# Gate and up projections of two feed-forward layers computed with seven block products

## The chip, the cores and the metric

The kernel runs on 1 core of one Trainium2 chip. The metric is the device time of one execution in microseconds (us). Three runs of the kernel before took 1439.99, 1441.54 and 1442.35 us; their median is 1441.54 us.

## The reference, cut to what matters

One layer of a hybrid decoder on 544 tokens (512 of a new sequence, 8 sequences of 4 new tokens): a half-step feed-forward layer, a mixer, a second half-step feed-forward layer, a gated per-layer embedding, a last norm. All of it is float32.

```python
def _swiglu(h, w_up, w_down):
    g, u = jnp.split(h @ w_up, 2, axis=-1)
    return (jax.nn.silu(g) * u) @ w_down

x = x + 0.5 * _swiglu(_rmsnorm(x, n_f1), w_f1u, w_f1d)      # w_up 1024 x 5632, w_down 2816 x 1024
m, new_conv, new_ssm, new_hg = _mixer(_rmsnorm(x, n_mix), ...)
x = x + m
x = x + 0.5 * _swiglu(_rmsnorm(x, n_f2), w_f2u, w_f2d)
gate = jax.nn.sigmoid(_rmsnorm(x, n_ple) @ w_ple_gate)
e = _rmsnorm(p @ w_ple_proj, ple_post)                      # p has 256 features
x = x + gate * e
y = _rmsnorm(x, norm_final)
```

The mixer also returns new recurrent states of the 8 sample sequences (`new_ssm`, `new_hg`): 32 blocks of 128x512 in, as many out.

## The kernel before

Tokens lie along the free dimension: x is held as 8 tiles of 128 features x 544 tokens, and a product's output is 128 features x 544 tokens in two PSUM banks of 272 columns each, the two halves. A float32 product is made of three matmuls in the reduced type: with a = hi + lo, it is hi·hi + hi·lo + lo·hi (`mm6`, L133: six matmuls of 272 columns for a 128x128 block of weights, three kinds by two halves). So every weight slab (`slab`, L117: one transfer of 512 KB into `wraw`) costs a cast on ScalarE (`whi`, L124) and a subtraction on VectorE (`wlo`, through `tt`, L54), both 128x1024, and every activation is split in the same way.

A feed-forward layer (`ffn`, L197) goes over 22 pairs j of a gate block and an up block. Each of the two is one slab, 8 blocks, 48 matmuls, so a pair has 96 matmuls into two `ps_up` tiles of the PSUM pool `big` (two tiles of two banks). Then VectorE multiplies both by the inverse norm r (`ft`), ScalarE does Silu, VectorE multiplies, and the product is split into `hh` and `hl`. All 22 pairs stay in SBUF; then the down projection (`ps_dn`) goes over 8 output tiles m with 22 blocks each in one PSUM sum, and adds half of it to x. A second PSUM pool, `sm` (4 banks, `ps_s`), serves small products.

Feed-forward layer 1 starts with the product of the per-layer embedding, `ps_e` (96 matmuls, from L280), made while x is loading; e is normed beside the up pairs (`e_sq`, `e_out`) and spilled to `es_d` in DRAM. In the mixer, input projections are `ps_in`, the output projection `ps_wo` (L791: 8 tiles m of 2 slabs). The updates of sample states (`ssm_update` L799, `hg_update` L832) are handed to the second layer's `ffn` as `extra` and run beside its up pairs. At the end come the gate's products (`ps_pg` and `ps_s`, L939; the first half of the columns for all m, then the second; `gh` and `gl` are the hi and lo parts of its weights) and the last norm (`final`, L895).

The code is recorded in program order and a scheduler then puts each engine's instructions in an order. Each engine, and SyncE's queue of transfers (SP), works through its own list in that order.

## Time and profile before

| | |
|---|---|
| median of 3 runs | 1441.54 us |
| profiled execution | span 1439.4 us |
| PE busy | 1421.3 us, 99% |
| DVE, ACT, POOL busy | 797.4, 542.1, 84.2 us (55, 38, 6%) |
| DMA | 159.43 MB, mean 111 GB/s |
| chain that ended last | PE 96%, of the span `ps_up` 37%, `ps_in` 22%, `ps_dn` 18%, `ps_wo` 6% |
| `ps_up` matmuls | 4224 in all (1408 of each of three kinds) |

The span is the time from the first to the last record of the profiled execution; the median of the runs is 2.1 us above it. PE is TensorE's matmuls, DVE is VectorE, ACT is ScalarE, POOL is GpSimd. Matmuls overlap in their pipeline, so the duration of one record (some 290 ns) is longer than its share of a chain.

### The profile page before, as it was taken

How to read it: one execution, taken by the hardware profiler on the slowest of the kernel's cores; microseconds unless marked ns; L12 is line 12 of the kernel's file. 1: busy time of each engine (PE TensorE's matmuls, PEld its weight loads, DVE VectorE, ACT ScalarE, POOL GpSimd, SP SyncE). 2: the span in 40 equal slices, each digit the busy share in tenths (PEclk: the TensorE clock that was granted, in tenths of full speed). 3: DMA queues.
4: the chain of work that ended last, by engine and by line, in shares of the span. 5: the costliest groups of instructions: out<-in, count | busy, mean ns of one | idle time of the engine just before them, and what ended most of it. 6: DMA issues, size and time to landing. Idle time of an engine off the chain costs nothing.

```text
span 1439.4 us, 26883 instructions
## 1 busy us (share of the span) xinstructions
PE 1421.3 (99%) x11461; PEld 1380.7 (96%) x11461; DVE 797.4 (55%) x1351; ACT 542.1 (38%) x841; POOL 84.2 (6%) x110
## 2 busy tenths in 40 slices
PE   8999999999999999999999999999999999999997
PEld 7999999999999999999999879999999999999997
DVE  6444544423237787777777466255676764322264
ACT  7322322222234355555555345233222222222264
POOL 2000000000101200000001021100000000000000
PEclk9999999999999999999999999999999999999998
DMA  6222422233331242322222352234455553232421
GB/s 212 89 88 88 136 89 88 85 91 114 114 121 60 90 137 92 92 92 90 92 91 99 98 173 74 88 107 125 163 191 168 169 176 96 81 96 81 142 90 63
DMA packets 58824, 159.43 MB, mean 111 GB/s; under 512 B 7568, under 2 KB 12816, under 8 KB 58704
## 3 DMA queue, kind: packets, MB, share of 16 engines
q1 hardware_dynamic: 57120, 155.10, 33.6%
q10 hardware_dynamic: 1584, 2.61, 0.5%
q8 instruction: 90, 1.47, 0.4%
q14 instruction: 30, 0.25, 0.1%
HBM read 140.93 MB, written 16.75 MB: 110 GB/s over the span
## 4 chain that ended last, share of the span: by engine, by line
PE 96%; ACT 1%; DVE 1%; DMA 1%; issue 0%; SPq 0%; DVEq 0%; ACTq 0%
PE ps_up L137 37%; PE ps_in L137 22%; PE ps_dn L137 18%; PE ps_wo L137 6%; PE ps_s L939 3%; PE ps_s L522 1%; PE ps_s L519 1%; PE ps_pg L939 1%; PE ps_s L499 1%; PE ps_s L632 1%; PE ps_s L495 1%; PE ps_s L162 0%; DMA x<-in_xT 0%; PE ps_s L170 0%; PE ps_s L648 0%; PE ps_s L644 0%
## 5 line engine op out<-in xcount | busy, mean ns | idle before, releaser
L124 ACT CAST whi<-wraw 128x1024 fp32r<-128x1024 f32 (+2 forms) x207 | 213.0, 1029 | 713.1 <-PE ps_up L137 305.4
L54 DVE TENSOR_TENSOR wlo<-wraw,whi 128x1024 fp32r<-128x1024 f32 (+2 forms) x207 | 248.5, 1200 | 173.4 <-ACT whi L124 170.5
L137 PE MATMUL ps_up<-xwl,whi 128*128 128x272 f32 x1408 | 292.3, 289 | 0.0
L137 PE MATMUL ps_up<-xwh,whi 128*128 128x272 f32 x1408 | 291.8, 288 | 0.3 <-ACT e L288 0.2
L137 PE MATMUL ps_up<-xwh,wlo 128*128 128x272 f32 x1408 | 291.5, 288 | 0.0
L137 PEld LDWEIGHTS ps_up<-xwh,whi 128*128 128x128 f32 x1408 | 222.7, 188 | 2.0 <-ACT e L288 0.5
L137 PEld LDWEIGHTS ps_up<-xwl,whi 128*128 128x128 f32 x1408 | 222.0, 189 | 0.0
L137 PEld LDWEIGHTS ps_up<-xwh,wlo 128*128 128x128 f32 x1408 | 220.3, 188 | 0.0
L54 DVE TENSOR_TENSOR ft<-ps_up,r 128x544 f32<-128x544 f32 x88 | 63.7, 724 | 230.3 <-PE ps_up L137 222.7
L137 PE MATMUL ps_in<-xwh,whi 128*128 128x272 f32 x832 | 183.6, 298 | 0.0
L137 PE MATMUL ps_in<-xwh,wlo 128*128 128x272 f32 x832 | 175.6, 291 | 0.0
L137 PE MATMUL ps_in<-xwl,whi 128*128 128x272 f32 x832 | 175.1, 290 | 0.0
L137 PEld LDWEIGHTS ps_in<-xwh,whi 128*128 128x128 f32 x832 | 132.4, 189 | 8.5 <-issue 8.2
L137 PEld LDWEIGHTS ps_in<-xwh,wlo 128*128 128x128 f32 x832 | 131.5, 188 | 2.9 <-issue 2.9
L137 PE MATMUL ps_dn<-hl,whi 128*128 128x272 f32 x640 | 132.9, 289 | 0.0
L137 PEld LDWEIGHTS ps_in<-xwl,whi 128*128 128x128 f32 x832 | 131.3, 189 | 1.5 <-issue 1.5
L137 PE MATMUL ps_dn<-hh,wlo 128*128 128x272 f32 x640 | 132.6, 289 | 0.0
L137 PE MATMUL ps_dn<-hh,whi 128*128 128x272 f32 x640 | 132.4, 288 | 0.0
L137 PEld LDWEIGHTS ps_dn<-hh,wlo 128*128 128x128 f32 x640 | 100.8, 188 | 0.0
L137 PEld LDWEIGHTS ps_dn<-hh,whi 128*128 128x128 f32 x640 | 100.6, 188 | 0.0
L137 PEld LDWEIGHTS ps_dn<-hl,whi 128*128 128x128 f32 x640 | 100.3, 188 | 0.0
L54 POOL TENSOR_TENSOR sq<-sq 128x544 f32<-128x544 f32 x16 | 23.7, 1481 | 818.3 <-ACT sq L74 818.3
(323 smaller groups left out, 1852.9 us busy)
## 6 DMA issues: line engine op xcount, KB each, us to landing
wraw<-in_w_in SPq DMA_DIRECT2D x52, 512.0 KB, 3.4
wraw<-in_w1u SPq DMA_DIRECT2D x44, 512.0 KB, 3.3
wraw<-in_w2u SPq DMA_DIRECT2D x44, 512.0 KB, 3.4
wraw<-in_w1d SPq DMA_DIRECT2D x16, 512.0 KB, 3.5
h<-in_hssm SPq DMA_DIRECT2D x32, 256.0 KB, 2.9
wraw<-in_w_o SPq DMA_DIRECT2D x16, 512.0 KB, 3.8
wraw<-in_w2d SPq DMA_DIRECT2D x16, 512.0 KB, 3.5
s<-in_hhg SPq DMA_DIRECT2D x8, 512.0 KB, 3.7
```

Source lines behind the costliest of these rows:

```text
L54: (eng or V).tensor_tensor(out=out, in0=a, in1=b, op=op)
L124: A.copy(hi[:, s], raw[:, s])
L137: PE.matmul(ps[:m, hf, :HN], w, x[:, hf * HN:(hf + 1) * HN], start=start and n == 0, stop=stop and n == 2)
L495: PE.matmul(pi[32 * j:32 * j + 32], Cm[:, b], h0, start=b % 2 == 0, stop=b % 2 == 1, tile_position=(0, 32 * j))
L499: PE.matmul(pst, Bk, xef, start=True, stop=True)
L519: PE.matmul(py[64 * e:64 * e + 64, q * P:q * P + n], xdt[:n, 2 * q + e], E[:n, 2 * q + e, :n], start=True, stop=pi is None, tile_position= ...
L522: PE.matmul(py[:, q * P:q * P + n], yf[:, q * P:(q + 1) * P], cs("sel") if smpl else cs("ident"), start=False, stop=True)
L632: PE.matmul(pat[32 * j:32 * j + 32, c * P:(c + 1) * P], cw[:, c * P + 32 * j:c * P + 32 * j + 32], qs, start=True, stop=True, tile_positio ...
L939: PE.matmul(ps[:, :HN], w[k // 4][:, k % 4 * P:k % 4 * P + P], xw[k][x][:, sl], start=k == 0 and n == 0, stop=k == KD - 1 and n == 2)
```

## The change

Of 22 pairs the first (`up_plain`) is computed as before. For each of the others the gate and up blocks, [1024 features] x [128 gate, 128 up], and the activations, [544 tokens] x [1024 features], are seen as 2x2 blocks (features in two halves of 512, tokens in two halves of 272), and the four block sums come from seven block products instead of eight. A product is 4 blocks of three matmuls, 12 matmuls of 272 columns.

Sums and differences of blocks are needed on both sides. Of the activations (`strassen_x`): t1 to t4 on POOL, once per layer. Of the weights (`strassen_w`), for every pair: `wr1[4:8]` = r1 + r3 (POOL, 512 wide), `wsf` = r1 − r2 (DVE, 1024 wide), `wr3[4:8]` = r2 − sf (POOL, 512 wide), and hi and lo parts of r2, of `wr1[4:8]`, of `wsf` and of r3. On the result side ACT copies partial sums out of PSUM (`keep`: s1, s5, s2, s3, 272 wide), and DVE and POOL add. The products run through four banks of the pool `sm`, and the last product of a pair (`rest`) is put behind the second of the next.

The down projection is done in groups, after pairs 6, 12, 18 and at the end (6, 6, 6 and 4 pairs), each a PSUM sum of its own that is added to x. The embedding product e and its norm stand behind layer 2 instead of before layer 1, and the spill is gone. The state updates stand in the loop of `ps_wo`, two for each of 16 slabs.

```diff
-    def ffn(xs, nname, wu, wd, fp, pre, acc=None, extra=()):
-                for k in range(KD):
-                    mm6(ps, hi[:, k], lo[:, k], xw[k][0], xw[k][1], k == 0, k == KD - 1)
...
+    def strassen_w(src, fp, plain=False):
+        r1 = fp.tile([P, 8, P], F32, name="wr1", tag="wr1", bufs=2)
+        r2 = wp.tile([P, 8, P], F32, name="wraw", tag="wraw", bufs=2)
+        r3 = fp.tile([P, 8, P], F32, name="wr3", tag="wr3", bufs=2)
+        sf = fp.tile([P, 8, P], F32, name="wsf", tag="wsf", bufs=1)
+        nc.sync.dma_start(r2, src[:, 4:12])
+        nc.sync.dma_start(r1[:, 0:4], src[:, 0:4])
+        nc.sync.dma_start(r3[:, 0:4], src[:, 12:16])
...
+        g1 = cut(r2, wp, "")
...
+        tt(r1[:, 4:8], r1[:, 0:4], r3[:, 0:4], ALU.add, eng=G)
+        g2 = cut(r1[:, 4:8], fp, "2", 4, bufs=1)
+        tt(sf.rearrange("p (a b) c -> p a (b c)", a=2), r1.rearrange("p (a b) c -> p a (b c)", a=2),
+           r2[:, 0:4].rearrange("p b c -> p (b c)").unsqueeze(1).to_broadcast([P, 2, 512]), ALU.subtract)
+        g3 = cut(sf, fp, "3", bufs=2)
+        tt(r3[:, 4:8], r2[:, 4:8], sf[:, 4:8], ALU.subtract, eng=G)
+        g4 = cut(r3, wp, "")
+        return {1: (g1, 0), 2: (g1, 4), 5: (g2, 0), 7: (g3, 0), 6: (g3, 4), 4: (g4, 0), 3: (g4, 4)}
+
+    def product(ps, w, x, start):
+        (hi, lo), o = w
+        for k in range(4):
+            xh, xl = x[k // 2]
+            for n, (a, b) in enumerate(((lo, xh), (hi, xh), (hi, xl))):
+                PE.matmul(ps[:, :HN], a[:, o + k], b[:, k % 2], start=start and k == 0 and n == 0,
+                          stop=k == 3 and n == 2, skip_group_check=not start)
...
+        def up(j):
+            w = strassen_w(wu[j], fp)
+            a, e = small(), small()
+            product(a, w[1], X[1], True)
+            s1 = keep(a, "s1")
...
+            product(e, w[5], X[5], True)
+            s5 = keep(e, "s5")
+            while late:
+                late.pop()()
+            d = small()
+            product(d, w[2], X[2], True)
+            g = fp.tile([P, T], F32, name="g", tag="g", bufs=2)
+            tt(g[:, :HN], s1, d[:, :HN], ALU.add)
+            product(a, w[6], X[6], False)
+            s2 = keep(a, "s2")
+            product(e, w[3], X[3], False)
+            tt(g[:, HN:], s2, e[:, :HN], ALU.add)
+            r = rr[0]
+            tt(g, g, r, ALU.mult)
+            sg = g
+            act(sg, g, AF.Silu)
+            tt(sg, sg, r, ALU.mult, eng=G)
+            product(a, w[7], X[7], False)
+            s3 = keep(a, "s3")
+            tt(s5, s5, s3, ALU.add, eng=G)
+
+            def rest():
+                product(a, w[4], X[4], False)
+                tt(sg[:, :HN], sg[:, :HN], a[:, :HN], ALU.mult)
+                tt(sg[:, HN:], sg[:, HN:], s5, ALU.mult)
+                hh = fp.tile([P, T], F32R, name="hh", tag="h")
+                hl = fp.tile([P, T], F32R, name="hl", tag="h")
+                A.copy(hh, sg)
+                tt(hl, sg, f32(hh), ALU.subtract)
+                hs.append((hh, hl))
...
+        for j in range(1, NFF):
+            up(j)
+            if j and j % 6 == 0:
+                down(s0, j - s0)
+                s0 = j
...
+                    for g in begun:
+                        next(g, None)
+                    begun = [x() for x in ups[:2]]
+                    del ups[:2]
+                    for g in begun:
+                        next(g)
                 tt(h2(xt), ps[:, :, :HN], h2(xt), ALU.add)
...
+    with tc.tile_pool(name="f3", bufs=34, reuse_waits="tile") as fp:
...
+            ps = big.tile([P, 2, 512], F32, name="ps_e", tag="big")
...
+            e = eslot("e")
+            A.copy(h2(e), ps[:, :, :HN])
+            es.append(e)
```

**VectorE and GpSimd in the up phase.** Of the kernel before, one pair on VectorE in layer 1 (`ft` is a gate or up block, `hl` the split of their product):

```order
L54 TENSOR_TENSOR ft_1047<-ps_up_943,r_372 128x544
L54 TENSOR_TENSOR wlo_1117<-wraw_1115,whi_1116 128x1024
L54 TENSOR_TENSOR ft_1050<-ps_up_998,r_372 128x544
L54 TENSOR_TENSOR ft_1050<-ft_1047,ft_1050 128x544
L54 TENSOR_TENSOR wlo_1185<-wraw_1183,whi_1184 128x1024
L54 TENSOR_TENSOR hl_1054<-ft_1050,hh_1053 128x544
```

With the change, one pair on VectorE in the steady part of layer 1 (`g` is the pair's gate, later its product with up; `wsf`, `wr1`, `wr3` are raw weights and their sums):

```order
L54 TENSOR_TENSOR wlo_1812<-wr3_1791,whi_1811 128x1024
L54 TENSOR_TENSOR g_1742<-s2_1756,ps_s_1682 128x272
L54 TENSOR_TENSOR g_1742<-g_1742,r_318 128x544
L54 TENSOR_TENSOR g_1742<-g_1742,s5_1709 128x272
L54 TENSOR_TENSOR wlo3_1941<-wsf_1926,whi3_1940 128x1024
L54 TENSOR_TENSOR wsf_2060<-wr1_2057,wraw_2058 128x1024
L54 TENSOR_TENSOR wlo2_1936<-wr1_1923,whi2_1935 128x512
L54 TENSOR_TENSOR g_1742<-g_1742,ps_s_1681 128x272
L54 TENSOR_TENSOR wlo_1931<-wraw_1924,whi_1930 128x1024
L54 TENSOR_TENSOR hl_1860<-g_1742,hh_1859 128x544
L54 TENSOR_TENSOR g_1876<-s1_1829,ps_s_1863 128x272
```

and on GpSimd, over the same pair (the last row begins the next):

```order
L54 TENSOR_TENSOR g_1742<-g_1742,r_318 128x544
L54 TENSOR_TENSOR s5_1709<-s5_1709,s3_1786 128x272
L54 TENSOR_TENSOR wr1_2057<-wr1_2057,wr3_2059 128x512
L54 TENSOR_TENSOR wr3_2059<-wraw_2058,wsf_2060 128x512
L54 TENSOR_TENSOR g_1876<-g_1876,r_318 128x544
```

VectorE has eleven instructions to a pair where it had six, and GpSimd four where it had none: the gate's second product by r, after Silu, the sum s5 + s3 and two sums of raw weights. The weights' rows are those of the two pairs that follow. On ScalarE the copy s2, which the product M7 (into the same bank) waits for, stands behind `hh` of the pair before and behind a cast of weights.

**VectorE from the output projection into layer 2.** Before, around the last addition of `ps_wo` to x (`xwl` is the lo part of the activations):

```order
L57 SCALAR_TENSOR_TENSOR xwl_10507<-xb_9573,vec_67,xwh_10506 128x544
L57 SCALAR_TENSOR_TENSOR xwl_10511<-xb_9573,vec_67,xwh_10510 128x544
L54 TENSOR_TENSOR wlo_10589<-wraw_10587,whi_10588 128x1024
L57 SCALAR_TENSOR_TENSOR xwl_10515<-xb_9573,vec_67,xwh_10514 128x544
L54 TENSOR_TENSOR xb_9573<-ps_wo_10352,xb_9573 128x544
L54 TENSOR_TENSOR wlo_10663<-wraw_10661,whi_10662 128x1024
L54 TENSOR_TENSOR sq_10463<-sq_10463,sq_10483 128x544
L57 SCALAR_TENSOR_TENSOR xwl_10519<-xb_9573,vec_67,xwh_10518 128x544
```

With the change:

```order
L54 TENSOR_TENSOR xb_9844<-ps_wo_11017,xb_9844 128x544
L54 TENSOR_TENSOR h0_11080<-h0_11080,ps_s_11157 128x512
L54 TENSOR_TENSOR s0_11095<-s0_11095,ps_s_11161 128x512
L54 TENSOR_TENSOR h0_11165<-h0_11165,ps_s_11179 128x512
L54 TENSOR_TENSOR s0_11170<-s0_11170,ps_s_11183 128x512
L54 TENSOR_TENSOR sq_11187<-sq_11187,sq_11207 128x544
L165 RECIPROCAL ra_11411<-ra_11411 128x5
L61 TENSOR_SCALAR b11_11227<-xb_9844,vec_67 128x272 x2
L54 TENSOR_TENSOR bl_11231<-b11_11227,bh_11230 128x544
L54 TENSOR_TENSOR b12l_11238<-b12_11234,b12h_11237 128x544
L61 TENSOR_SCALAR b11_11243<-xb_9844,vec_67 128x272 x2
L54 TENSOR_TENSOR wlo2_11299<-wr1_11287,whi2_11298 128x512
```

The splits of activations stood among the last tiles of `ps_wo`; now every block of layer 2 (`b11`, `b12h`, `bl` and, further on, those of b21, b22 and t1 to t4) stands behind the last state update.

**ScalarE at the end.** Before, around the gate's weights:

```order
L74 ACTIVATE sq_14884<-xb_9573 128x544
L883 CAST gh_14906<-wraw_14910 128x512
L883 CAST gh_14907<-wraw_14910 128x512
L883 CAST gh_14916<-wraw_14920 128x512
L883 CAST gh_14917<-wraw_14920 128x512
L883 CAST gh_15011<-wraw_15015 128x512
L883 CAST gh_15012<-wraw_15015 128x512
L74 ACTIVATE xwh_14859<-xb_9573,vec_67 128x544
L883 CAST gh_15055<-wraw_15059 128x512
```

With the change, the same place:

```order
L1033 COPY e_15691<-ps_e_15678 128x544
L74 ACTIVATE sq_15927<-e_15661 128x544
L74 ACTIVATE sq_15930<-e_15676 128x544
L1033 COPY e_15706<-ps_e_15693 128x544
L74 ACTIVATE sq_15933<-e_15691 128x544
L74 ACTIVATE sq_15935<-e_15706 128x544
L1033 COPY e_15721<-ps_e_15708 128x544
L74 ACTIVATE sq_15938<-e_15721 128x544
L1033 COPY e_15736<-ps_e_15723 128x544
L74 ACTIVATE sq_15941<-e_15736 128x544
L1057 CAST gh_15944<-wraw_15948 128x512
```

The copies of `ps_e` out of PSUM, one for each of 8 tiles, and the squares of e now stand between the casts of the gate's first slabs and those of the others.

## Rows read from the trace of the kernel before

**Rows 1.** The chain of waits on the page (part 4): shares of the span by engine.
```profile
PE 96%; ACT 1%; DVE 1%; DMA 1%; issue 0%; SPq 0%; DVEq 0%; ACTq 0%
```

**Rows 2.** Windows: window, length, busy us of each engine (count), PEclk, DMA share, GB/s.
```profile
0.00:21.00 21.00, 14.21 (x96) 13.54 (x96) 13.07 (x18) 15.50 (x24) 0.45 (x6) 1.00 0.73 264
964.00:1240.00 276.00, 275.48 (x2160) 273.89 (x2159) 170.97 (x291) 81.14 (x107) 0.00 (x0) 1.00 0.47 151
1240.00:1374.00 134.00, 134.00 (x1064) 134.00 (x1064) 39.98 (x45) 34.86 (x44) 8.18 (x6) 1.00 0.35 106
1374.00:1439.40 65.40, 55.28 (x440) 54.86 (x438) 38.39 (x87) 36.39 (x72) 2.70 (x2) 0.93 0.19 65
```

**Rows 3.** Chain of waits in order of time: start us, length us, what.
```profile
4.50 6.39 DMA x<-in_xT
...
21.06 7.55 PE ps_up L137 x58
...
291.31 132.96 PE ps_dn L137 x1056
...
963.79 6.05 PE ps_up L137 x48
...
1240.60 133.27 PE ps_dn L137 x1056
1373.88 6.70 PE ps_pg L939 x53
...
1389.92 16.27 PE ps_s L939 x130
```

**Rows 4.** DVE groups by form; after the bar: busy us, mean ns of one, idle before.
```profile
L54 DVE TENSOR_TENSOR wlo<-wraw,whi 128x1024 fp32r<-128x1024 f32 x189 | 231.9, 1227 | 172.8 <-ACT whi L124 169.8
L54 DVE TENSOR_TENSOR ft<-ps_up,r 128x544 f32<-128x544 f32 x88 | 63.7, 724 | 230.3 <-PE ps_up L137 222.7 <-ACT r L173 7.3
...
L54 DVE TENSOR_TENSOR gt<-gt,e 128x272 f32<-128x272 f32 x16 | 6.9, 439 | 4.0 <-ACT gt L74 3.7
```

**Rows 5.** DVE timeline in the first 21 us; first column is the start.
```profile
12.96 0.72 DVE L54 TENSOR_TENSOR sq<-sq 128x544 f32<-128x544 f32 x1
13.59 0.78 DVE L57 SCALAR_TENSOR_TENSOR xwl<-x,vec,xwh 128x544 fp32r<-128x544 f32 x1
...
19.37 1.22 DVE L54 TENSOR_TENSOR wlo<-wraw,whi 128x1024 fp32r<-128x1024 f32 x1
20.50 0.78 DVE L57 SCALAR_TENSOR_TENSOR xwl<-x,vec,xwh 128x544 fp32r<-128x544 f32 x1
```

**Rows 6.** ACT groups by form.
```profile
L124 ACT CAST whi<-wraw 128x1024 fp32r<-128x1024 f32 x189 | 198.4, 1050 | 656.4 <-PE ps_up L137 305.4 <-issue 113.0 <-PE ps_in L137 95.9
...
L74 ACT ACTIVATE ft<-ft 128x544 f32<-128x544 f32 x44 | 29.0, 660 | 2.1 <-DVE ft L54 2.1
...
L883 ACT CAST gh<-wraw 128x512 fp32r<-128x512 f32 x16 | 9.3, 616 | 10.9 <-DMA wraw<-in_w_pg 8.5 <-PE ps_dn L137 2.2
...
L288 ACT COPY e<-ps_e 128x544 f32<-128x544 f32 x4 | 2.4, 606 | 0.2 <-PE ps_e L137 0.2
...
L915 ACT COPY rs<-ps_f 128x272 f32<-128x272 f32 x2 | 0.8, 386 | 2.7 <-PE ps_f L912 2.7
```

**Rows 7.** POOL groups by form.
```profile
L54 POOL TENSOR_TENSOR xb<-xb,rs 128x544 f32<-128x544 f32 x2 | 2.7, 1352 | 71.0 <-ACT rs L915 71.0
```

**Rows 8.** POOL timeline around 849 us.
```profile
848.78 2.03 POOL L54 TENSOR_TENSOR f<-f,sg 128x544 f32<-128x544 f32 x1 [5.02 <-ACT sg L74]
850.77 1.35 POOL L54 TENSOR_TENSOR q<-q,sg 128x544 f32<-128x544 f32 x1
```

**Rows 9.** DVE timeline of the same stretch.
```profile
848.38 1.22 DVE L54 TENSOR_TENSOR wlo<-wraw,whi 128x1024 fp32r<-128x1024 f32 x1
...
850.96 1.74 DVE L54 TENSOR_TENSOR cT<-cT,f 128x544 f32<-128x544 f32 x1
```

**Rows 10.** The page's DMA issues (part 6): KB each, median us from issue to landing.
```profile
wraw<-in_w2u SPq DMA_DIRECT2D x44, 512.0 KB, 3.4
```

More of the change, by code (lines that the diff above doesn't have):

```diff
@@ new lines, in strassen_x, with slot, put, block @@
+    def strassen_x(xs, nname, fp):
+        ops = {}
+        spare = [fp.tile([P, 2, HN], F32R, name="bh2" if i % 2 else "bl2", tag="xw2", bufs=12) for i in range(12)]
+        def slot(nm):
+            return fp.tile([P, 2, HN], F32, name=nm, tag="h")
+        def put(key, i, t):
+            n = len([1 for v in ops.values() for x in v if x])
+            if n < 8:
+                hi = xwp.tile([P, 2, HN], F32R, name="bh", tag="xw", bufs=16)
+                lo = xwp.tile([P, 2, HN], F32R, name="bl", tag="xw", bufs=16)
+            else:
+                lo, hi = spare.pop(0), spare.pop(0)
+            A.copy(hi, t)
+            tt(lo, t, f32(hi), ALU.subtract)
+            ops.setdefault(key, [None, None])[i] = (hi, lo)
+        def block(k0, half, nm):
+            t = slot(nm)
+            for q in range(2):
+                src, n = xs[k0 + q][:, half * HN:(half + 1) * HN], vc(nname, k0 + q)
+                if half:
+                    act(t[:, q], src, AF.Copy, scale=n)
+                else:
+                    ts(t[:, q], src, n, ALU.mult)
+            return t
+        b12, t1, b21, b22 = [], [], [], []
+        plain = []
+        for i in range(2):
+            b11 = block(2 * i, 0, "b11")
+            put(1, i, b11)
+            b = block(2 * i, 1, "b12")
+            hi = fp.tile([P, 2, HN], F32R, name="b12h", tag="h")
+            lo = fp.tile([P, 2, HN], F32R, name="b12l", tag="h")
+            A.copy(hi, b)
+            tt(lo, b, f32(hi), ALU.subtract)
+            plain.append((hi, lo))
+            b12.append(b)
+            t = slot("t1")
+            tt(t, b, b11, ALU.subtract, eng=G)
+            t1.append(t)
+        for i in range(2):
+            b21.append(block(4 + 2 * i, 0, "b21"))
+            put(2, i, b21[i])
+            b22.append(block(4 + 2 * i, 1, "b22"))
+            put(3, i, b22[i])
+        def combos():
+            for i in range(2):
+                put(5, i, t1[i])
+            for i in range(2):
+                t2 = slot("t2")
+                tt(t2, b22[i], t1[i], ALU.subtract, eng=G)
+                put(6, i, t2)
+                t3 = slot("t3")
+                tt(t3, b12[i], b22[i], ALU.subtract, eng=G)
+                put(7, i, t3)
+                t4 = slot("t4")
+                tt(t4, b21[i], t2, ALU.subtract, eng=G)
+                put(4, i, t4)
+        return ops, plain, combos
@@ L246, in body @@
+        s0 = 0
+        first = up_plain()
+        next(first)
+        combos()
+        for j in range(1, NFF):
[3 more added lines that the diff above has]
+                s0 = j
+        while late:
+            late.pop()()
+        down(s0, NFF - s0)
     x_sp = dram.tile([KD, P, T], F32, name="x_sp")
-    es_d = dram.tile([KD, P, T], F32, name="es_d")
     acs_d = dram.tile([5, 16, P], F32, name="acs_d")
@@ L309, in body, with load_x @@
+    with tc.tile_pool(name="f1", bufs=18, reuse_waits="tile") as fp:
+        xs = []
+        def load_x(ks):
+            for k in ks:
+                t = fp.tile([P, T], F32, name=f"x{k}", bufs=1)
+                nc.sync.dma_start(t, xT[k])
+                xs.append(t)
+        load_x(range(2))
+        w0 = strassen_w(w1u[0], fp, True)
+        load_x(range(2, KD))
+        nc.sync.dma_start(cst, csts)
+        ffn(xs, "n_f1", w1u, w1d, fp, w0=w0)
         for k in range(KD):
@@ L942, in body @@
                     r = rms_r(acc_x)
+                if hf == 0 and m in (2, 4):
+                    next(eg)
                 if hf == 1 and m in (1, 2):
```

350 lines of the change are left out of this document (178 added, 172 removed).

## The prediction

> **What bounds the kernel now.** I read the chain of waits first. Nearly all of it is PE [rows 1], so a matmul taken out of the chain is worth its whole interval, and any other engine costs something only where it makes PE wait. The chain in order of time gives the interval: in the down projections 1056 matmuls of 272 columns in 132.96 us, 0.126 us each, and 130 matmuls of the gate, with the operands of one half alone as in the new products, 0.125 us each [rows 3]. The windows by stage then say what lies beside PE: in the second layer's up stage DVE works 171 of 276 us, ACT 81, POOL nothing [rows 2]. The groups and timelines of DVE, ACT and POOL [rows 4 to 9] give the prices. The profiled execution has a span of 1439.4 us; the median of the runs is 2.1 us longer, and I carry that difference along.
>
> **1. Fewer matmuls.** In 21 of 22 pairs 84 matmuls stand for 96. 2 layers x 21 x 12 = 504, by 0.126 us [rows 3]: **−63.5 us**, if PE never waits. The matmuls of the down groups, of e and of the state updates are as many as before; each m of a group has a bank sum of its own, which adds 24 per layer to the 8 DVE additions into x. Such a PSUM addition is near the 0.72 us of the 544-wide PSUM product [rows 4], and a group's m has 36 matmuls, 4.5 us, above it: hidden. This is the only term that gains.
>
> **2. The up pairs in the steady part.** PE's step shrinks from 96 to 84 intervals, 12.1 to 10.6 us, while the work beside it grows. From one start to the next DVE needs 1.13 us for 1024 wide, 0.63 for 544 [rows 5]; 512 and 272 wide I take in proportion at 0.6 and 0.36, the latter a little under its 0.44 us record [rows 4]. DVE's eleven instructions are four of 1024, one of 512, two of 544 and four of 272: 4.5 + 0.6 + 1.3 + 1.4 = 7.8 us. Of these, three 272-wide ones read PSUM. POOL took 1.35 us for 544 wide [rows 7], so in proportion 1.27 for each of two sums of 512 and 0.68 for 272: 4.6 us a pair. ACT has three casts of 1024, one of 512, `hh`, Silu and four copies from PSUM: 3 x 1.05 + 0.62 + 2 x 0.66 + 4 x 0.39 [rows 6] = 6.6 us. Each alone fits under 10.6.
>
> Two things don't fit. First, DVE waits inside its own queue. Between g·r and g·s5 lie Silu on ACT (0.66) and two POOL instructions (1.35 + 0.68), 2.7 us in which nothing else of DVE's queue can go ahead; 7.8 + 2.7 = 10.5 us, just under PE's step. Second, DVE and POOL exclude each other. At 848.78 POOL began a 544-wide product while a DVE subtraction from two SBUF tiles ran from 848.38 to 849.60; POOL took 2.03 instead of 1.35 us. Then POOL began at 850.77 and DVE's 544-wide product at 850.96 took 1.74 us instead of 0.7, ending 0.6 us after POOL did [rows 8, 9]. So whichever came first held the other off for its whole length. The Trainium skill says the same of the cause ("SBUF — State Buffer", Who interferes with whom): a VectorE instruction with two SBUF inputs and a GpSimd instruction that reads SBUF exclude each other; by that rule alone, without the order of the queues, a pair needs the sum of both, some 11.2 us, and the loss of this part would be (11.2 − 10.6) x 42 = 25 us, a floor that lets nothing be regained.
>
> With the order of the queues it is more. I follow DVE from the end of g·r: Silu and POOL's two instructions to 2.7; POOL's next, the sum `wr1`, has its loads and takes the port to 4.0; g·s5 4.3, `wlo3` 5.5, `wsf` 6.6, `wlo2` 7.2; then g·a reads PSUM, and POOL's `wr3`, which waited for `wsf`, goes in from 7.2 to 8.45; `wlo` 9.6, `hl` 10.2, g+d 10.6, `wlo` 11.7, g+e 12.1, g·r **12.7**. Without the exclusion 10.5. PE cannot run ahead of it: M7 needs the copy s2, on ACT s2 stands behind `hh`, and `hh` waits for g·a and g·s5 of the pair before. So each step is 2.1 us late once the loop governs. In a group of six the first two pairs have the lead of the down group before them, and in the last two DVE has no new weights to make (the following slabs come after those of the down projection), which leaves about 0.2 + 2.1 + 2.1 + 1.0 = 5.4 us. Three groups of six in two layers: **+33 us** with the short last group. Bounds: +3 if POOL's sums always find DVE idle or reading PSUM, +55 if four or five steps of six are late.
>
> **3. The start.** Before, PE began `ps_up` at 21.06 us, having made e while x landed [rows 3]. Now PE has no e to make, but block conversions: 8 half-scalings on each of DVE and ACT, 16 casts and 16 subtractions of 544, 8 sums on POOL at 1.35, and the first weights. DVE's part until the second pair can run is some 16 x 0.63 + 8 x 0.36 + 6 weight instructions, 19 us, POOL's 10.8 us excluding it in places. With the loads at the rate of the first stretch (264 GB/s [rows 2]) x and the first 1 MB are in at about 13 us. I expect PE's steady part to begin as if its first pair had started at 28: **+7** (−4 if conversions keep up with the loads, +12 if POOL's sums and DVE's subtractions alternate).
>
> **4. The start of layer 2.** Before, `ps_up` follows at 963.79 with no gap [rows 3], since the splits of x were made tile by tile. Now everything, b11 first, stands behind the last state update, and `wr1` and `wr3` of the first pair are loaded from SP's queue behind the updates' last results, 3.4 us to landing [rows 10]. PE waits some 5.5 us for the first block; then DVE has some 13 us of work until the last block of the first pair (which is 12.1 us of PE) and 7 more, with t1 to t4 on POOL beside it, before the second pair has all of its operands. **+17** (+6 if only the first wait shows, +23).
>
> **5. The end.** e's 96 matmuls lie now on the chain between the last `ps_dn` and `ps_pg`: 12.1 us. There are two PSUM tiles for 8 products, and each waits for an ACT copy (0.61 [rows 6]) that stands among gate casts (0.62 each) and squares (0.65). From 1374 ACT works 36 of 65 us already [rows 2]. `ps_pg`, in the same two tiles, waits for the copies; I put it 18 us later than 1373.88 [rows 3], and 3 us more are for e's norm and eight scalings, which hold the gate's first products. **+21** (+12 for the matmuls alone, +28).
>
> **6. The output projection.** A slab has 48 matmuls, 6.05 us [rows 3], and gains two updates, 2 x (256 KB in, 256 KB out) beside its 512 KB: 1.5 MB in some 6.4 us is 240 GB/s, where the first 21 us show 264 at a share of 0.73 [rows 2]. Tight but possible; the 32 small matmuls only change place. **+2** (0 … +10).
>
> **Sum.** −63.5 + 33 + 7 + 17 + 21 + 2 = +16.5: a span of 1456 us, a median of **1458 us**. About 0.2%, 2.9 us, can be told from no change.
>
> **The rivals.**
> *A, faster: the loop of DVE and POOL does not govern.* Place: DVE's queue in the up pairs. If POOL's two weight sums fall into the 2.7 us where DVE waits or beside its PSUM reads, the step stays PE's 10.6. The other losses would then shrink too, as the same exclusion is in them: −63.5 + 3 + 3 + 10 + 16 + 0 = −31.5, **1410 us**. It decides at the point where terms 3 to 6 (47) leave 16.5 us for 42 pairs, 0.4 us a pair: a mean step below 11.0 us is faster, above it slower. For it speaks that POOL is idle through the second layer's up stage [rows 2], so it may run early; against it, that 2.7 us are already POOL's own and that the bare sum of both engines is above 11.0. Chance 0.37.
> *B, much slower: PE's clock falls.* With steps of 12.7 us PE is busy 83% of the time. The one stage of that kind, the last, with 55.28 of 65.40 us (85%), has a granted clock of 0.93 [rows 2]. If up pairs get this, their PE work of 42 x 10.6 us grows by 7%, 31 us, perhaps two thirds of it seen, since DVE's loop is the longer: 1458 + 20 = **1478 us**. Chance 0.11.
> *C, no difference.* The step is 11 us, and terms 3 to 6 take the rest of the gain: **1441 us**, chance 0.08.
>
> **How the numbers follow.** The forecast, 1458, has 0.44, with a range of its own of 1446 to 1474. Faster is A, 0.37; same is C, 0.08; slower is the forecast and B, 0.55. The range reaches from a little under A to a little over B: 1406 to 1484, which leaves out 2 in 10 (no loss at all beside PE, and the upper ends of terms 2 to 5 together).
>
> **What would show it.** Right: in the up stages PE busy some 85 to 90% with gaps that end at DVE `g` or ACT s2; POOL's 512-wide sums and DVE's `wlo` of well over 1.27 and 1.23 us; a gap of about 5 us before layer 2's first `ps_up`; `ps_pg` some 18 us behind the last `ps_dn`. Wrong: steps of 10.6 us between the pairs with PE at 99%, or POOL's and DVE's means as in the kernel before.

## The result and the profile after

Four runs of the changed kernel took 1496.55 to 1499.31 us, median **1497.53 us**; four of the kernel before beside them had a median of 1441.36. The ratio is 1.0389 [1.0375, 1.0404]: slower, as forecast, but by 56 us where 16.5 were forecast, and beyond the upper end of the range (1484). The page of the changed kernel, its engines, two rows of its slices and the group of matmuls with the longest idle time:

```profile
span 1496.2 us, 27222 instructions
...
PE 1407.9 (94%) x10997; PEld 1358.5 (91%) x10997; DVE 1037.1 (69%) x1592; ACT 695.6 (46%) x1210; POOL 345.1 (23%) x304
...
PE   5899999999999999999999989978999998999897
PEclk8999999999999999999999999978999999999898
...
L315 PE MATMUL ps_s<-bh,wlo 128*128 128x272 f32 x1176 | 349.2, 297 | 39.7 <-ACT s L326 34.0
```

PE was busy 1421.3 us before. With 504 matmuls fewer it should be busy some 63 us less and is busy 13 less: where it had waited, it then ran at the lower of its two clock levels for a while (the low digits of `PEclk`), and a matmul there takes longer. The last row is the loop that the prediction described: the product M7 waits for the copy s2 (`s`, L326). The chain of waits of this execution is followed back only to 1276 us, so its shares can't be set against those of [rows 1]; I cut both traces at the first and last matmuls of each stage instead. In us, with two of the experiments below:

| stage | before | after | e3_all4 | h1_two |
|---|---|---|---|---|
| start to layer 1's last `ps_dn` | 424.1 | 423.0 | 398.3 | 391.5 |
| mixer | 437.7 | 440.4 | 438.6 | 438.5 |
| output projection | 101.8 | 118.6 | 118.3 | 116.2 |
| wait before layer 2's `ps_up` | 0 | 8.2 | 8.5 | 8.4 |
| layer 2 to its last `ps_dn` | 410.1 | 408.8 | 381.3 | 377.8 |
| rest, to the end | 65.7 | 97.3 | 97.2 | 96.1 |

The two layers, in which 42 pairs have 12 matmuls fewer each, gain 2.4 us together; the output projection, the wait behind it and the end lose 56.6. The windows of the changed kernel show the kind of loss in each place (columns as in [rows 2]): the start, one full group of layer 1 and 3.5 us within it, the output projection, the start of layer 2, the end and 13.7 us within it:

```profile
24.00:42.00 18.00, 9.62 (x46) 9.30 (x45) 17.79 (x12) 7.09 (x12) 15.78 (x9) 0.62 0.11 36
151.10:221.40 70.30, 65.41 (x494) 64.75 (x493) 49.85 (x60) 32.54 (x55) 24.88 (x20) 0.95 0.27 83
171.20:174.70 3.50, 3.37 (x15) 3.38 (x16) 3.17 (x5) 0.33 (x2) 0.00 (x0) 0.51 0.59 186
863.40:982.00 118.60, 112.39 (x839) 108.95 (x838) 87.44 (x139) 58.13 (x117) 30.45 (x22) 0.97 0.68 216
987.00:1020.00 33.00, 26.39 (x139) 24.25 (x140) 30.52 (x32) 19.08 (x35) 19.25 (x11) 0.69 0.25 78
1398.90:1496.20 97.30, 80.41 (x578) 79.47 (x576) 53.64 (x109) 55.72 (x108) 11.60 (x8) 0.86 0.20 67
1403.50:1417.20 13.70, 12.02 (x54) 12.02 (x55) 6.43 (x10) 6.71 (x12) 1.63 (x1) 0.50 0.11 39
```

At both starts (first and fifth row) DVE is busy 17.79 of 18 and 30.52 of 33 us and PE's clock is at 0.62 and 0.69; in the full group PE loses some 8.7 us of 70. Part of DVE's busy time at the starts is time in which POOL held it off: three `bl` took 5.41 us while POOL made its t sums, where one takes 0.71 us with POOL idle.

```profile
29.17 5.41 DVE L54 TENSOR_TENSOR bl<-t,bh 128x544 fp32r<-128x544 f32 x3
...
40.25 0.71 DVE L54 TENSOR_TENSOR bl<-t,bh 128x544 fp32r<-128x544 f32 x1
```

**One step of the loop.** VectorE in that group (L54; start, duration):

```profile
171.74 0.42 DVE L54 TENSOR_TENSOR g<-s,ps_s 128x272 f32<-128x272 f32 x1
172.09 1.21 DVE L54 TENSOR_TENSOR wlo<-wr,whi 128x1024 fp32r<-128x1024 f32 x1
173.22 0.42 DVE L54 TENSOR_TENSOR g<-s,ps_s 128x272 f32<-128x272 f32 x1
173.68 0.72 DVE L54 TENSOR_TENSOR g<-g,r 128x544 f32<-128x544 f32 x1
177.32 1.52 DVE L54 TENSOR_TENSOR g<-g,s 128x272 f32<-128x272 f32 x1 [2.91 <-POOL s L54]
...
181.81 0.43 DVE L54 TENSOR_TENSOR g<-g,ps_s 128x272 f32<-128x272 f32 x1
182.16 1.98 DVE L54 TENSOR_TENSOR wlo<-wraw,whi 128x1024 fp32r<-128x1024 f32 x1
...
184.70 0.42 DVE L54 TENSOR_TENSOR g<-s,ps_s 128x272 f32<-128x272 f32 x1
```

and GpSimd over the end of the step before and this one:

```profile
162.16 1.29 POOL L54 TENSOR_TENSOR wr<-wr,wr 128x512 f32<-128x512 f32 x1 [4.59 <-DMA wr<-in_w1u]
163.40 1.36 POOL L54 TENSOR_TENSOR g<-g,r 128x544 f32<-128x544 f32 x1
...
175.18 1.37 POOL L54 TENSOR_TENSOR g<-g,r 128x544 f32<-128x544 f32 x1 [5.08 <-ACT g L74]
176.50 0.78 POOL L54 TENSOR_TENSOR s<-s,s 128x272 f32<-128x272 f32 x1
177.24 1.30 POOL L54 TENSOR_TENSOR wr<-wr,wr 128x512 f32<-128x512 f32 x1
181.38 1.68 POOL L54 TENSOR_TENSOR wr<-wraw,wsf 128x512 f32<-128x512 f32 x1 [2.83 <-DVE wsf L54]
```

From g+d at 171.74 to the next at 184.70 is a step: 12.96 us; 12.7 were predicted. Its parts are those of the prediction: DVE waits for Silu and two POOL instructions, then g·s5 takes 1.52 us because POOL's weight sum began 0.08 us ahead of it, and the subtraction at 182.16 takes 1.98 because POOL's other sum had begun at 181.38. The row at 181.81, which reads PSUM and one SBUF tile, lies wholly beside that sum and takes its usual 0.43. The groups show the same as means:

```profile
L54 DVE TENSOR_TENSOR wlo<-wraw,whi 128x1024 fp32r<-128x1024 f32 x114 | 154.2, 1353 | 7.7 <-ACT whi L124 5.2 <-ACT whi L290 1.4
...
L54 DVE TENSOR_TENSOR g<-g,s 128x272 f32<-128x272 f32 x42 | 43.3, 1030 | 123.1 <-POOL s L54 115.6 <-POOL g L54 7.5
...
L54 DVE TENSOR_TENSOR g<-g,ps_s 128x272 f32<-128x272 f32 x42 | 18.0, 429 | 2.8 <-PE ps_s L315 2.8
L54 POOL TENSOR_TENSOR wr<-wraw,wsf 128x512 f32<-128x512 f32 x42 | 65.2, 1551 | 226.2 <-DVE wsf L54 199.6 <-issue 18.2 <-ACT whi L290 8.4
L54 POOL TENSOR_TENSOR wr<-wr,wr 128x512 f32<-128x512 f32 x42 | 62.2, 1481 | 81.2 <-DMA wr<-in_w1u 30.2 <-DMA wr<-in_w2u 25.9 <-DVE g L54 10.7
```

1030 ns where [rows 4] had 439 for the same width, and DVE 123.1 us idle ahead of g·s5, 2.9 a pair. New is what stands at 162.16: the sum of the pair after next, ahead of g·r in POOL's queue, waits 4.59 us for its loads.

### The profile page after: what moved, and what is told of

It reads as the page before. It is cut to its first block, busy times and chain, and to the rows that moved or that the text cites. A ratio compares the mean times of both kernels' runs of the same rounds, so it can differ in the third digit from the quotient of the medians.

```text
span 1496.2 us, 27222 instructions
## 1 busy us (share of the span) xinstructions
PE 1407.9 (94%) x10997; PEld 1358.5 (91%) x10997; DVE 1037.1 (69%) x1592; ACT 695.6 (46%) x1210; POOL 345.1 (23%) x304
## 5 line engine op out<-in xcount | busy, mean ns | idle before, releaser
L315 PE MATMUL ps_s<-bh,wlo 128*128 128x272 f32 x1176 | 349.2, 297 | 39.7 <-ACT s L326 34.0
L315 PE MATMUL ps_s<-bh,whi 128*128 128x272 f32 x1176 | 345.9, 294 | 0.0
L315 PE MATMUL ps_s<-bl,whi 128*128 128x272 f32 x1176 | 345.1, 293 | 0.0
L315 PEld LDWEIGHTS ps_s<-bh,wlo 128*128 128x128 f32 x1176 | 228.8, 195 | 44.5 <-ACT s L326 38.3
L124 ACT CAST whi<-wraw 128x1024 fp32r<-128x1024 f32 (+2 forms) x134 | 123.4, 921 | 298.7 <-PE ps_dn L137 96.6
L315 PEld LDWEIGHTS ps_s<-bh,whi 128*128 128x128 f32 x1176 | 229.2, 195 | 0.0
L315 PEld LDWEIGHTS ps_s<-bl,whi 128*128 128x128 f32 x1176 | 229.0, 195 | 0.0
L54 DVE TENSOR_TENSOR wlo<-wraw,whi 128x1024 fp32r<-128x1024 f32 (+2 forms) x178 | 210.8, 1185 | 10.5 <-ACT whi L124 8.0
L54 DVE TENSOR_TENSOR g<-g,s 128x272 f32<-128x272 f32 x42 | 43.3, 1030 | 123.1 <-POOL s L54 115.6
L54 POOL TENSOR_TENSOR wr<-wraw,wsf 128x512 f32<-128x512 f32 x42 | 65.2, 1551 | 226.2 <-DVE wsf L54 199.6
```

The source lines that it names most:

```text
L54: (eng or V).tensor_tensor(out=out, in0=a, in1=b, op=op)
L124: A.copy(hi[:, s], raw[:, s])
L315: PE.matmul(ps[:, :HN], a[:, o + k], b[:, k % 2], start=start and k == 0 and n == 0, stop=k == 3 and n == 2, skip_group_check=not start)
```

## The experiments

Three questions: what makes the groups of pairs long (DVE and POOL on each other, the clock, POOL's queue); what the starts, the output projection and the end cost by themselves; and whether a version is left that gains. Times are medians of 4 to 10 runs, ratios to the kernel before on the same chip.

**The loop: two instructions at a time.** The weights' sums on DVE:

```diff
-        tt(r1[:, 4:8], r1[:, 0:4], r3[:, 0:4], ALU.add, eng=G)
+        tt(r1[:, 4:8], r1[:, 0:4], r3[:, 0:4], ALU.add)
...
-        tt(r3[:, 4:8], r2[:, 4:8], sf[:, 4:8], ALU.subtract, eng=G)
+        tt(r3[:, 4:8], r2[:, 4:8], sf[:, 4:8], ALU.subtract)
```

> The two sums of raw weights (512 wide, wr1 and wr3) go from GpSimd to VectorE; gate product and s5 + s3 stay on GpSimd. Theory (GpSimd and VectorE exclude each other, and VectorE waits in its own queue): a pair needs 7.8 + 1.2 us on VectorE and 2.7 us of waiting for Silu and GpSimd, 11.7 instead of the 12.95 us measured with the change, the gaps of PE fall from 2.4 to about 1.1 us, and the clock no longer falls in the groups: each full group some 5 us shorter, 1497 becomes about 1468. Rival (what counts is VectorE's own work): a pair becomes 1.2 us longer, 1497 becomes about 1520 or more.

Measured: 1469.56 us, 1.0187 [1.0163, 1.0210], as the theory had it (1468); a full group takes 64.8 to 65.4 us. The two of the gate on DVE instead:

```diff
-            tt(sg, sg, r, ALU.mult, eng=G)
+            tt(sg, sg, r, ALU.mult)
...
-            tt(s5, s5, s3, ALU.add, eng=G)
+            tt(s5, s5, s3, ALU.add)
```

> The gate's second product by r and s5 + s3 go from GpSimd to VectorE; the sums of raw weights stay on GpSimd. Theory: VectorE has 8.9 us of work and waits only for Silu, 0.7; GpSimd's sums, 2.5 us, exclude it for some 1.5 to 2.5 us, 11.1 to 12.1 us a pair: 1497 becomes 1465 to 1480. Rival (VectorE's own work counts): a pair 1.0 us longer, about 1520.

Measured: 1464.83 us, 1.0161 [1.0145, 1.0176], at the lower end of the theory (1465); a full group takes 64.0 us. Both edits together:

> All four GpSimd instructions of a pair go to VectorE, GpSimd has nothing in the steady part. Theory: VectorE has 10.05 us of work and waits 0.7 for Silu, 10.75 us a pair, near PE's own 10.6: the groups lose 1 to 2 us instead of 8, 1497 becomes about 1455. Rival (VectorE's own work counts): 12.95 + 2.2 = 15.2 us a pair, 1497 becomes 1560 or more.

Measured: 1442.84 us, 1.0005 [0.9995, 1.0015], 54.7 below the changed kernel and 12 below the 1455 of the theory, which had still let the groups lose 1 to 2 us. The full group of layer 1 in the windows, and two of DVE's groups:

```profile
143.73:205.30 61.57, 61.57 (x494) 61.57 (x493) 53.94 (x80) 32.88 (x55) 0.00 (x0) 1.00 0.30 95
```

```profile
L54 DVE TENSOR_TENSOR wlo<-wraw,whi 128x1024 fp32r<-128x1024 f32 x114 | 142.1, 1247 | 10.0 <-ACT whi L290 4.9 <-ACT whi L124 4.0
...
L54 DVE TENSOR_TENSOR g<-g,s 128x272 f32<-128x272 f32 x42 | 18.3, 437 | 0.6
```

DVE has more to do in the group (53.94 us, not 49.85), POOL nothing, and PE never waits: 492 matmuls in 61.6 us, 0.125 each. g·s5 is back at 437 ns. So the work that the change put on POOL cost 55 us, and DVE had room for it.

**The clock.** In the changed kernel a matmul behind one of these waits takes 0.227 us for 3.4 us. Twelve products that nobody reads are put into the wait of three pairs of each full group, 216 matmuls in all:

```diff
...
+            if j % 6 in (2, 3, 4) and j < 19:
+                warm = big.tile([P, 2, 512], F32, name="warm", tag="big")
+                (hi, lo), o = w[3]
+                for k in range(12):
+                    ins = PE.matmul(warm[:, 0, :HN], hi[:, o], X[3][0][0][:, 0], start=k == 0, stop=k == 11)
+                    after(ins, m3)
+                    m3 = ins
...
```

> The change as it is, and twelve matmuls more (1.5 us, their result is not used) in the three pairs of each full group in which PE waits, just before the product that waits for the copy s2. They cover 1.5 of the 2.4 us in which PE is idle, so the clock should stay at its upper level there. In the change nine windows at the lower level lie in the up groups, 34 us in all, in which PE loses some 17 us of progress. Theory (the loop over VectorE and GpSimd governs; PE's slow stretch is mostly swallowed by its next wait): only the last slow stretch of a group is gained, 6 groups x 1.7 us, 1497 becomes 1487 to 1493. Rival (the clock is what makes the groups long): all 17 us are gained, about 1480. A third (matmuls added to the chain cost their time): 18 x 1.5 = 27 us more.

Measured: 1500.10 us, 1.0405 [1.0389, 1.0421], none of the three. The same group here:

```profile
152.70:223.30 70.60, 67.15 (x530) 66.26 (x529) 46.63 (x60) 32.30 (x55) 25.05 (x20) 1.00 0.27 81
```

The granted clock is 1.00 (0.95 in the changed kernel), and the group is as long. Behind the twelve products PE still waits for the copies, 3.4 us in this group (4.9 in the changed kernel), so it was not their own time that ate a gain of the clock. The lower clock goes with the waits, and products that run faster only wait longer for the next copy: the loop sets the length. Over all groups the up stages are 6 us longer here, the end, which the edit leaves as it was, 3.4 shorter (more on this under term 5).

**POOL's queue.** In each of the four full groups (pairs 7 to 12 and 13 to 18 of both layers) the first step from g·r to g·r takes 14.0 to 14.3 us, the next some 13.0, 13.0, 10.9 and 10. The weights' sum is put behind the g·r that it had held up:

```diff
-        tt(r1[:, 4:8], r1[:, 0:4], r3[:, 0:4], ALU.add, eng=G)
+        wsum = G.tensor_tensor(out=r1[:, 4:8], in0=r1[:, 0:4], in1=r3[:, 0:4], op=ALU.add)
+        after(wsum, turns[-2] if len(turns) > 1 else None)
...
-            tt(sg, sg, r, ALU.mult, eng=G)
+            turns.append(G.tensor_tensor(out=sg, in0=sg, in1=r, op=ALU.mult))
```

> The changed kernel, with one order added on POOL: the sum r1 + r3 of the pair after next is put behind g*r of the pair that is in PE's hands, where in the changed kernel the first step of every group had it ahead of g*r and waiting for its loads (4.59 us at 162.16). In the changed kernel a full group has steps of DVE's g*r of 14.3, 13.0, 13.0, 10.9 and 10.2 us. If the waiting at the head of POOL's queue costs what it delays, the first step falls to about 11.7 us (g*r on POOL then comes 1.5 us behind DVE's g*r as in the other steps, not 4.0) and each of six full groups ends some 2 to 2.5 us earlier: 1483 to 1487 us. If only the exclusion of the two engines sets the step, the sum falls into DVE's work a little later and the group is as long as before: 1495 to 1500 us, with the first step at or above 13 us or the later ones longer.

Measured: 1492.54 us, 1.0353 [1.0336, 1.0371], between the two. In the profiled executions the two layers are 3.3 us shorter; another 4.3 come at the end, which the edit leaves as it was. GpSimd in the first and second step:

```profile
161.38 1.36 POOL L385 TENSOR_TENSOR g<-g,r 128x544 f32<-128x544 f32 x1 [13.75 <-ACT g L74]
...
163.42 1.29 POOL L303 TENSOR_TENSOR wr<-wr,wr 128x512 f32<-128x512 f32 x1
...
175.30 1.37 POOL L385 TENSOR_TENSOR g<-g,r 128x544 f32<-128x544 f32 x1 [1.35 <-ACT g L74]
```

Nothing waits for loads any more, yet the steps are 13.4, 12.7, 12.4, 12.4 and 9.3 and the group 68.5 us: of the 8.0 to 8.7 us that a full group loses, the order of POOL's queue has 1.1 to 1.8. The rest is the exclusion and DVE's waits for POOL inside its own queue. The first two experiments part them roughly: 61.5 us with nothing on POOL (e3_all4), 64.8 to 65.4 with only the gate's two instructions there, for which DVE waits, 64.0 with only the weights' sums, which hold it off, 69.5 to 70.2 with all four.

**The starts.** t1 to t4 made on DVE, in the changed kernel (one of four lines alike):

```diff
-                tt(t2, b22[i], t1[i], ALU.subtract, eng=G)
+                tt(t2, b22[i], t1[i], ALU.subtract)
```

> Only t1 to t4, eight 544-wide sums at the start of each layer, go from GpSimd to VectorE; the pairs stay as in the change. Theory: GpSimd's 8 x 1.35 us and the VectorE subtractions beside them hold each other off at both starts, and on VectorE a sum takes 0.63 us: each start 5 to 8 us shorter, 1497 becomes 1482 to 1488. Rival (the starts are bound by loads and ScalarE): no change, or 5 us longer per layer.

Measured: 1494.62 us, 1.0369 [1.0353, 1.0384]: 3 us, a miss. The time to the first `ps_dn` is 2.1 us longer in layer 1 and 2.8 shorter in layer 2. DVE is held off less (busy 14.57 of the 18 us from 24 on, not 17.79) and waits 3.18 us for the norm instead; what sets the length of the starts this run doesn't show. From e3_all4 on (each of the following is e3_all4 with one more edit, or with several where it says so), t2 to t4 ahead of the squares for x's norm:

```diff
+            combos()
             ac = rms_two(xs, fp) if acc is None else [acc]
...
-        combos()
```

> On top of e3_all4: in each layer's start the sums t2 to t4 are put ahead of the squares for the norm. Theory (the first pairs wait for GpSimd's and VectorE's queue of sums, in which the squares stand first): layer 1's second pair starts some 5 us earlier, layer 2 gains nothing since its squares stand earlier, 1443 becomes about 1438. Rival (all of it has to be done by the same time anyway, r included): no change within 2 us.

Measured: 1446.68 us, 1.0030 [1.0017, 1.0043], 4 slower, in the start of layer 1. Then more matmuls in the time of the conversions: a second pair without block sums in each layer, at 12 more matmuls.

```diff
-        first = up_plain()
-        next(first)
+        first = [up_plain(jj) for jj in range(2)]
+        for f in first:
+            next(f)
         combos()
-        for j in range(1, NFF):
+        for j in range(2, NFF):
```

(The first pair's two PSUM tiles are copied out, so that the second can use them.)

> On top of e3_all4: in each layer the first two pairs are computed with the plain eight block products instead of the first alone (24 matmuls more in all, 3 us), and the first pair's two sums are copied out of PSUM before the norm is known. Theory (PE is idle from 24.8 to some 41 us and again in layer 2 because the second pair needs t1 to t4 and their splits, while a plain pair needs only blocks that are there): each start gains 8 to 10 us, 1443 becomes 1424 to 1430, below the kernel before. Rival (VectorE's total work, blocks and weights, sets the time by which the following pairs run): each start gains less than 2 us, 1439 to 1446.

Measured: **1432.71 us, 0.9937 [0.9922, 0.9951]**: 10 us below e3_all4 and 8.9 below the kernel before. By the table of stages layer 1 ends 6.8 us earlier and layer 2 takes 3.5 less, under the 8 to 10 expected of each start.

**The output projection.** e3_all4 without the 32 state updates (two outputs, the new states, are not computed):

```diff
-                    ups.append(lambda g=g, b=b: ssm_update(xp, g, b, st))
-                    ups.append(lambda h=b, hf=g: hg_update(xp, h, hf, st))
+                    pass
```

> On top of e3_all4, with the 32 state updates left out altogether (the two sample-state outputs are not computed): what they cost beside the output projection. Their own 32 matmuls are some 11 us. Theory (besides that they make PE wait at the projection's start, where slabs of w_o queue behind their loads, and hold up the first weights and blocks of layer 2): the output projection falls from 118 to 102 us and the wait before the first ps_up from 8 to 3 to 4 us, 1443 becomes about 1421. Rival (only their matmuls cost): 1443 becomes about 1432.

Measured: 1419.38 us, 0.9846 [0.9829, 0.9862]. The output projection here:

```profile
836.30:938.10 101.80, 101.55 (x810) 101.15 (x808) 41.02 (x49) 35.52 (x47) 12.00 (x7) 1.00 0.24 81
```

101.8 us at full clock, as before the change, and the wait before layer 2 falls from 8.5 to 3.7. So all 16.5 us are the updates. The changed kernel's first four slabs take 40.7 us (29.3 before); with the updates begun two slabs later,

```diff
-                    begun = [x() for x in ups[:2]]
-                    del ups[:2]
+                    si = 2 * m + n
+                    nu = 0 if si < 2 else 3 if si in (4, 6, 8, 10) else 2
+                    begun = [x() for x in ups[:nu]]
+                    del ups[:nu]
```

> On top of e3_all4: the state updates beside the output projection begin with the third slab instead of the first (three each at four slabs, two at the others). In e3_all4 the first four slabs of ps_wo take 41 us, in the kernel before some 26. Theory (the slabs of w_o stand in SP's queue behind the updates' loads and results): the first four slabs take 30 us or less, the rest some 3 us more, 1443 becomes 1434 to 1438. Rival (the start of ps_wo waits for the mixer's last tiles and the updates only change place): no change within 3 us.

it was 1447.43 us, 1.0045 [1.0030, 1.0060]: those slabs took 32.0, but the whole projection 120.3 and the wait behind it 11.8. The wait only moved.

**The end.** e's products put among the slabs of the output projection, the results kept in DRAM until the end (in short):

```diff
+                if m in (3, 7):
+                    e_prod(m // 4)
...
+            for m in range(KD):
+                e = eslot("e")
+                nc.sync.dma_start(e, es_d[m])
+                es.append(e)
```

> On top of e3_all4: the embedding product e is made in the output projection's loop (half after the fourth tile of ps_wo, half after the last), written to DRAM as it is, and read back at the end, where its squares, norm and scaling stay. Theory (e's 96 matmuls and their copies, with PE at its lower clock, are what the end lost: 97.2 us from the last ps_dn to the end of the span against 65.5 before): the end falls to 70 to 75 us, the output projection gains 12 us of matmuls, of which some 4 fill PE's wait at the start of layer 2: 1443 becomes 1424 to 1430. Rival (the end is long through the squares and scaling of e and the gate's casts): the end keeps over 85 us and the kernel stays at 1440 to 1447.

Measured: 1453.57 us, 1.0077 [1.0062, 1.0092]. The end shrank by 6.6 us to 90.6, the projection grew by 10.6 to 128.9; the rival was right on the end, and the total is worse than either had it. The same products behind layer 1's first pair, with e's norm beside its down groups:

```diff
         next(first)
+        if gap:
+            gap()
         combos()
```

> On top of e3_all4: the product e is made in layer 1 behind the first pair, where PE is idle from 24.8 to some 41 us, written to DRAM; its squares are summed beside the first down group, it is scaled beside the second, and read back at the end. Theory (of the end's 97 us the product, the norm and the scaling of e on the chain are some 25): the end falls to 72 to 76 us, the start grows by 2 to 4 us for VectorE's part, 1443 becomes 1420 to 1427. Rival (as in f2_early, the norm of x holds the end as long): the end keeps over 85 us, 1434 or more.

Measured: 1443.52 us, 1.0013 [1.0004, 1.0023]: the end 80.1 instead of 97.2, but layer 1 ends at 415.1 instead of 398.3. The time to the first `ps_dn` grew by 13.5 us, more than the 12 us of the 96 matmuls: PE has free time there, but nothing of them was hidden. That the products need casts and copies of the engines that were late already is the likely reason, not a shown one. A longer last group of downs:

```diff
-            if j and j % 6 == 0:
+            if j in (5, 10, 15):
```

> On top of e3_all4: the down groups are cut at 5, 5, 5 and 7 pairs instead of 6, 6, 6 and 4, so that an output tile of the last group has 42 matmuls, 5.3 us, instead of 24, 3.0 us. Theory (the end waits for the norm of x: beside 3.0 us of PE a tile's addition, split, square and the weights' split keep VectorE busy 2.9 us, so squares are left over, and PE's norm matmuls stand ahead of ps_e in its queue): the wait between the last ps_dn and ps_e falls from 6.8 to 2 us or less and the clock stays up, 1443 becomes 1433 to 1437. Rival (the end is long through e alone): no change within 2 us.

Measured: 1442.79 us, 1.0011 [1.0001, 1.0020], no change; the end 96.2. Both edits:

> g1_last7 and g2_front together. Theory: both waits at the end go, the end comes near the 65.5 us of the kernel before, 1443 becomes 1412 to 1420, below the kernel before. Rival (they are the same wait): no better than the better of the two.

Measured: 1442.18 us, 1.0007 [0.9997, 1.0016], no better than g1_last7 alone; end 79.8. And g3_both with x's norm on PE held behind the gate's first two products:

```diff
-                    r = rms_r(acc_x)
+                    r = rms_r(acc_x, gm)
```

> g3_both with the norm of x at the end held behind the gate's first two products on PE, as it stood in the kernel before. Theory (the 80 us that the end kept without e, against 65.5, come from the norm's matmuls, which stand ahead of ps_pg in PE's queue and wait for the squares, and from the clock that falls in that wait): the first ps_pg follows the last ps_dn within 1 us instead of 5.6, the end falls to 70 to 74 us, 1442 becomes 1433 to 1437. Rival (the end waits for r whatever the order): the end keeps 78 us or more, 1440 to 1443.

Measured: 1440.52 us, 0.9991 [0.9981, 1.0000]; end 77.4, and `ps_pg` still begins 5.5 us behind the last `ps_dn`. The order of PE's queue is not what holds the gate then. All of it together, with the second plain pair:

> h1_two and h2_norm together, with e's product behind the second plain pair. If both theories hold: 1418 to 1428; if only the starts: 1427 to 1436; if neither, 1440 or more.

Measured: 1436.03 us, 0.9966 [0.9953, 0.9979]: better than g3_both by 6, but behind h1_two alone. The end is 18.6 us shorter than there, but layer 1 ends 20.6 later: e's products cost more in the start that the second plain pair also fills (16.8 without it, in g2_front).

## Why the prediction was right in sign and wrong in size

The terms as predicted, and as the stages of the changed kernel and e3_all4 give them. For 3 and 4, the time to the first `ps_dn` is set against its 588 matmuls (96 of the plain pair, 492 of the others) at 0.1254 us, 73.7 us, with the loop's share taken out by e3_all4.

| term | predicted | measured | from |
|---|---|---|---|
| 1 fewer matmuls | −63.5 | −63.5 | e3_all4's full groups: 0.125 us a matmul |
| 2 loop of the pairs | +33 | +51 | up stages of after less e3_all4: full groups 8.0 to 8.7 each, four of them 33; first groups 7.2 and 10.8 |
| 3 start of layer 1 | +7 | +7 | 106.2 − 73.7 = 32.5 in place of 21.1, less 4 that layer 1's up stage before lost too (270.1 us for 2112 at 0.126) |
| 4 start of layer 2 | +17 | +24 | 8.5 + 89.0 − 73.7 |
| 5 end | +21 | +32 | 97.3 − 65.7 |
| 6 output projection | +2 | +6 | 118.6 − 101.8 = 16.8, less 10.7 us that layer 2 gave up |

They add to +56.5. With the mixer's +2.7, which no term has, it is 59.2, and the spans differ by 56.8: the terms are good to some 2 us. The 40 us between forecast and result are term 2 with 18, term 5 with 11, term 4 with 7 and term 6 with 4.

**Term 2, the loop: mechanism right, size wrong.** The step of 12.7 us was measured at 12.96, the two places of the exclusion were found where the prediction had them, and taking POOL's instructions away took the loss away. What failed is "the first two pairs have the lead of the down group before them". The first step of a group is the longest, 14.3 us, not one within the lead; so a group loses 8.0 to 8.7 us instead of 5.4, with PE busy 65.41 of 70.30 us, 93% (85 to 90 predicted). Part of that, 1.1 to 1.8 us, is the order of POOL's queue (i1_turn): that the sum `wr1` "has its loads" did not hold in the first step, where it waited 4.59 us for them. The bound of +55 had allowed for four or five late steps of six; it was three, but the first of them 3.7 us late where 2.1 were reckoned for a step. The floor that the prediction had estimated by the rule of the Trainium skill ("SBUF — State Buffer", Who interferes with whom), the bare sum of both engines, was 25 us. The measured loss of 51 is above it, and e3_all4 shows that it is gone without GpSimd's instructions.

**Term 3, the start of layer 1: right by luck.** PE's steady part began as if its first pair had started at 32.5 us, not at 28. The difference is still +7, because the kernel before lost some 4 us in its own up stage, which the prediction had not seen.

**Term 5, the end.** "e's 96 matmuls lie now on the chain" was right, but at 12.1 us they were priced at full clock and as if they could begin at once. The chain of the changed kernel shows what stood between:

```profile
1377.04 21.82 PE ps_dn L137 x172
...
1398.88 1.21 ACT sq L74 x2
...
1400.16 1.35 POOL sq L54
...
1403.36 1.78 POOL sq L54
...
1405.18 0.59 PE ps_s L162 x2
1405.77 2.93 PE ps_e L137 x12
...
1416.11 9.56 PE ps_e L137 x72
1425.67 6.05 PE ps_pg L1108 x48
```

x's norm (L162) stands ahead of `ps_e` in PE's queue and waits for POOL's squares: 6.3 us without a matmul; and from 1403.5 on the clock is 0.50, so a dozen of `ps_e` takes 2.93 us, not 1.5. `ps_pg` comes 26.8 us behind the last `ps_dn` (18 predicted). Of the 31.5 us, e has 17 (g2_front); the other 14 stayed when e was gone, with a longer last group (g1_last7, g3_both), and 12 of them with another order on PE (h2_norm). The lower clock has a part: in i1_turn and f1_fill, with the same code here, it lasted 6.8 us instead of 13.7, and `ps_pg` came 22.6 us behind the last `ps_dn`, 4 us earlier. The trace of h2_norm shows where its 12 us lie. PE's longest wait there is for ScalarE's casts of the gate's weights:

```profile
PE ps_pg L1135 <- ACT gh L1080: 5.4, 1, 5.4
```

ScalarE in the kernel before, where the last `ps_dn` ends at 1373.9, and below it in h2_norm, where that ends at 1363.0:

```profile
1368.48 1.14 ACT L883 CAST gh<-wraw 128x512 fp32r<-128x512 f32 x2 [6.30 <-DMA wraw<-in_w_pg]
1369.77 1.14 ACT L883 CAST gh<-wraw 128x512 fp32r<-128x512 f32 x2
```

```profile
1364.41 3.37 ACT L74 ACTIVATE sq<-xb 128x544 f32<-128x544 f32 x6
1367.68 2.16 ACT L1080 CAST gh<-wraw 128x512 fp32r<-128x512 f32 x4
```

Before, the first casts were done while PE still had `ps_dn`; in h2_norm they stand behind six squares of x, though their load had landed by 1349.4. The first 132 or so matmuls of the gate are through 16.1 us behind the last `ps_dn` before, 27.0 in h2_norm (at a clock of 0.78), and what follows takes 49.4 and 50.2 us. No run puts the casts ahead of the squares, so what that order is worth is not shown.

**Term 4, the start of layer 2.** DVE alternates with POOL's t sums as said, and DVE is busy 30.5 of 33 us; the first wait was 8.2 us instead of 5.5, and PE then had a clock of 0.69. With the t sums on DVE (e4_starts) this start is 2.8 us shorter, so moving them off POOL wins back little; that all of x is late at once is what remains, and no run parts it from DVE's own work.

**Term 6.** "the 32 small matmuls only change place" is right, but the sum didn't say that 10.7 us of layer 2 (276.8 us for 2112 matmuls of 0.126) move with them; the 6 us beyond are waits of the updates, which f3_none removes and g4_late only moves.

**The rivals.** A (1410 us) had asked that the loop not govern; e3_all4 makes just this true, and gets 1442.84: its second half, that the other losses shrink too, did not come with it. Terms 3 to 6 are there without any exclusion in the loop (the t sums at the starts are still on GpSimd in e3_all4). B's clock did fall (0.95 to 0.98 in the full groups), but as f1_fill shows it took no time from the groups; at the end it did, where the chain runs over `ps_e` at the lower level.
